# Moving the low part of the FFN's inner rows to another start address in SBUF

## The chip, the cores and the metric

The kernel runs on one core of a Trainium2 chip. The metric is the device time of one execution in microseconds, taken as the median of repeated runs. Before the change it is 2266.62 us (three runs, 2265.76 to 2267.56).

## The reference, cut to what matters

One decoder layer is computed for 256 prompt rows and 32 sample rows, 288 rows together, with a model width of 2048 and an FFN width of 5632:

```python
def ffn_half(h, g, wg, wu, wd):
    hn = rms_norm(h, g)
    return h + 0.5 * ((jax.nn.silu(hn @ wg) * (hn @ wu)) @ wd)

h = ffn_half(h, ...)            # half-step FFN 1
h = mixer_out(h, conv, attn)    # short convolution and forgetting attention, one output projection
h = ffn_half(h, ...)            # half-step FFN 2
h = ple_add(h, p, ...)          # sigmoid gate times a projection of the layer's input embedding
y = rms_norm(h, norm_final)
```

All data is float32. The "inner rows" are `silu(hn @ wg) * (hn @ wu)`, the input of the third FFN product. Only their place in memory is touched here.

## The kernel before, in words

**Three products for one.** The activations lie transposed: 128 features on the partitions, the 288 rows along the free dimension. Each float32 operand of the large products is split into a high part that the matmul's reduced format (float32r) holds exactly and a low part, the rest. A product is then three matmuls that add into one PSUM bank: low activation times high weight, high activation times high weight, high activation times low weight. The first two are line 338 of the profile (`mm<-...,whi`), the third is line 340 (`mm<-...,wlo`). Such a group of three is called a *triplet* below. The activation is the moving operand (128 x 288), the weight the stationary one (128 x 128); every matmul has its own weight load, which runs beside the matmul ahead of it.

**Loops.** `pair` makes two blocks of 128 output features from blocks of 128 input features, four input blocks ("chunk") at a time: for each of the two outputs and each of the four inputs one triplet. Its usual order is low, high, high. The argument `rows_first`, used for the first gate and up pair of FFN 1 while weights still arrive, takes high, low, high, with the same three weights in the order high, high, low.

**The FFN.** The 5632 inner features are 44 blocks. They are made in groups of 6, 6, 8, 8, 8, 8 blocks: for each group the gate and up products with `x` as the moving operand, then the down product over this group's blocks with `hid` as the moving operand, added into `h`. `up` writes a block of `hid`: line 417 (ScalarE) rounds to the high part, line 418 (VectorE) takes the difference. The tile `hid` is made anew for each group, with two buffers.

**Addresses.** A tile's place decides where its parts start. In the built program `hid` begins at byte 129504 of each partition, which is 224 modulo 256, and `x` at byte 38944, which is 32 modulo 256. `both` leaves a gap in front (7 elements for `hid`, 55 for `x`), so that in both the first high part starts at 252 modulo 256. Block k holds the high part, 288 elements or 1152 bytes, and the low part right behind it; a block takes 2304 bytes, nine times 256, so every high part starts at 252 and every low part at 124 modulo 256. The weights' tiles `whi` start at 0 and `wlo` at 224 modulo 256, and a load's columns at multiples of 512 bytes from there. The tiles of the convolution group's output (`zc`) and of the input embedding (`ph`) are made by `both` too, at 252 and 124. The attention group's outputs, `zah` and `zal`, are plain tiles: high parts at 224, low parts at 96.

**The order of work.** The program is recorded by Python loops and placed by a scheduler; TensorE runs its instructions in that order. Weight tiles come in through a queue on SP and are split into `whi` and `wlo` by line 292 (ScalarE and VectorE).

Of the kernel before, what the change touches and what calls it, by code (L numbers as in the profile page):

```python
# [17 lines left out]
F32R = mybir.dt.float32r  # L18
# [7 lines left out]
P = 128  # L26
# [6 lines left out]
NT = SEQ + NS  # L33
# [11 lines left out]
HALVES = 5  # L45
BEFORE_X = 55
BEFORE_W = 7
MANUAL = False
BANKS = dict(mm=3, kt=3, va=2)
KPAIRS = (1, 8, 14, 21, 27, 34, 40, 47)  # L50
# [44 lines left out]
def build(nc, tc, ctx, A, O):  # L95
# [3 lines left out]
    v, s, g, pe, sy = nc.vector, nc.scalar, nc.gpsimd, nc.tensor, nc.sync  # L99
# [99 lines left out]
    def norm_scale(out, squares, width, chunks, load=False):  # L199

        s.activation(sqh, squares, AF.Copy)
        v.tensor_tensor(sql, squares, sqh.bitcast(F32), ALU.subtract)
        defer(lambda: inv_rms(out, [sqh, sql], width, load), chunks)
# [4 lines left out]

    X = {}

    def both(p, name, blocks, before, **k):
        n = blocks * 2 * NT
        whole = 64 if k else 8
        t = p.tile([P, -(-(before + n) // whole) * whole], F32R, name=name, tag=name, **k)
        t = t[:, before:before + n].rearrange("p (k s n) -> p s k n", s=2, n=NT)
        return t[:, 0], t[:, 1]

    def new_x():
        X["hi"], X["lo"] = both(xp, "x", KT, BEFORE_X)

    def make_x(k, gname, work):

        split(X["hi"][:, k, :], X["lo"][:, k, :], h[:, k, :], gain(gname, k))
        squares(k, work)
# [132 lines left out]
    def run_steps():  # L357
        for its, _ in steps:
            items.extend(its)
            for it in its:  # L360
                if it["kind"] == "w":
                    halves.extend((it, j) for j in range(0, it["nk"], 2))
        for i in range(0, 16, 4):
            halves[i + 1], halves[i + 2] = halves[i + 2], halves[i + 1]
        for its, fn in steps:
            load_upto(state["used"] + state["ahead"])
            fn()
            state["used"] += len(its)

    def do(fn):  # L370
        steps.append(([], fn))
# [18 lines left out]
    def ffn(wg, wu, wd, nextgain, work):  # L390
        npairs = DFF // 256
        groups = [range(0, 3), range(3, 6)] + [range(p, p + 4) for p in range(6, npairs, 4)]
        H = {}
        for gi, grp in enumerate(groups):
            firstg = gi == 0 and nextgain == "norm_mix"

            def start():
                H["hi"], H["lo"] = both(work(), "hid", 8, BEFORE_W, bufs=2)
            do(start)
            for pi, pr in enumerate(grp):  # L400
                sg = {}

                def gate(b, o, sg=sg):
                    w = work()
                    t = w.tile([P, NT], F32, name="tg", tag="tg", bufs=2)
                    v.tensor_tensor(t, o, rs, ALU.mult)  # L406
                    u = w.tile([P, NT], F32, name="sg", tag="sg", bufs=2)
                    s.activation(u, t, AF.Silu)  # L408
                    r = w.tile([P, NT], F32, name="sr", tag="sr", bufs=3)
                    g.tensor_tensor(r, u, rs, ALU.mult)  # L410
                    sg[b] = r

                def up(b, o, sg=sg, pi=pi):
                    t = work().tile([P, NT], F32, name="hd", tag="hd", bufs=2)
                    v.tensor_tensor(t, o, sg[b], ALU.mult)  # L415
                    k = 2 * pi + b
                    s.activation(H["hi"][:, k, :], t, AF.Copy)  # L417
                    v.tensor_tensor(H["lo"][:, k, :], t, H["hi"][:, k, :].bitcast(F32), ALU.subtract)  # L418

                lead = firstg and pi == 0  # L420
                gs = pair(wg, pr * 256, list(range(KT)), xact, gate, **(dict(late=4 if lead else 2, tag="va", rows_first=lead) if pr == 0 else {}))
                us = pair(wu, pr * 256, list(range(KT)), xact, up, **(dict(late=4, tag="kt", rows_first=True) if lead else {}))
                steps.extend([x for gu in zip(gs, us) for x in gu] if lead else gs + us)
            k0 = grp[0] * 2
            nb = 2 * len(grp)
            lastg = gi == len(groups) - 1
            for ob in range(KT // 2):
                def down(b, o, ob=ob, lastg=lastg):
                    k = 2 * ob + b
                    v.scalar_tensor_tensor(h[:, k, :], o, 0.5, h[:, k, :], ALU.mult, ALU.add)  # L430
                    if lastg:
                        if k == 0:
                            new_x()
                        make_x(k, nextgain, work())
                steps.extend(pair(wd, ob * 256, list(range(k0, k0 + nb)),
                                  lambda k: (H["hi"][:, k, :], H["lo"][:, k, :]), down, k_of=lambda k, k0=k0: k - k0))
        do(lambda: norm_scale(rs, acc, D, 3, True))
# [484 lines left out]
    def state_in():  # L922
        M["st"] = W["zq"][0].tile([P, CB, DB, 2], F32, name="st")
        M["zc"] = both(W["zq"][0], "zc", CB, BEFORE_W)
        g.dma_start(M["st"].rearrange("p i b t -> p i (b t)"), A["state"])
# [184 lines left out]
    def ple_start():  # L1110
# [4 lines left out]
        g.dma_start(pa, A["p"])  # L1115
        E["hi"], E["lo"] = both(w, "ph", 2, BEFORE_W)
        for k in range(2):
# [61 lines left out]
    do(finish)  # L1179
    with (tc.manual_schedule(engines={mybir.EngineType.PE}) if MANUAL else ExitStack()):  # L1180
        run_steps()
# [67 lines left out]
```

## Time and profile before

| what | us |
|---|---|
| median of three runs | 2266.62 |
| profiled execution, its own time | 2266.11 |
| span of the profiled execution, first to last instruction | 2264.3 |
| TensorE busy in the span | 2250.4 |
| VectorE busy | 1342.5 |
| ScalarE busy | 1047.3 |
| GpSimd busy | 323.0 |

There are 17,387 matmuls in the profile. Of the triplets, 3680 read `x` into the `mm` banks and 1408 read `hid`; `zc` has 128, `zah` and `zal` together 128, `ph` 32, and 160 more read `x` into other banks. A matmul's duration in the profile (290 to 293 ns) is longer than its spacing from the next, because matmuls are pipelined; the time of a stretch is read from starts and counts, not from durations. The timeline prints starts to a hundredth of a microsecond, so a spacing is taken over many matmuls.

### The profile page before, as it was taken

What the parts mean: (1) busy time and instruction counts of PE and PEld (TensorE: products, weight loads), DVE (VectorE), ACT (ScalarE), POOL (GpSimd) and SP (SyncE); (2) the same over time, 40 slices, a digit from 0 to 9 for tenths busy, and PEclk for the clock granted to TensorE, in tenths of its full rate; (3) what the DMA queues carried; (4) which work ended last, traced back from release to release, by engine and by line L of the source; (5) the groups of instructions that cost most, each with busy time, mean ns of one, the idle gap of its engine ahead of it and who ended that gap; (6) DMA issues with size and microseconds to landing.
All of it is one profiled execution on the core that took longest, in us unless ns stands there. A gap on an engine that the chain in (4) does not pass through costs nothing.

```text
span 2264.3 us, 44311 instructions
## 1 busy us (share of the span) xinstructions
PE 2250.4 (99%) x17387; PEld 2194.2 (97%) x17387; DVE 1342.5 (59%) x2413; ACT 1047.3 (46%) x1860; POOL 323.0 (14%) x398
## 2 busy tenths in 40 slices
PE   9999999999999999999999999999999999999997
PEld 9999999999999999888888999999999999999997
DVE  7555555555555586456567875555555555555865
ACT  6444444444444553334344554444444444444654
POOL 1020000000000013345446210000000000000210
PEclk9999999999999999999999999999999999999999
DMA  8575555555555556988988555555555555555552
GB/s 278 169 245 169 170 174 168 168 169 171 172 169 168 168 168 238 332 300 302 331 323 301 167 171 159 179 162 182 168 168 168 174 170 170 168 169 172 169 171 94
DMA packets 342865, 443.37 MB, mean 196 GB/s; under 512 B 17424, under 2 KB 307104, under 8 KB 342656
## 3 DMA queue, kind: packets, MB, share of 16 engines
q1 hardware_dynamic: 320944, 366.25, 50.6%
q0 software_dynamic: 20480, 71.67, 8.9%
q8 instruction: 136, 2.23, 0.4%
q10 hardware_dynamic: 1232, 2.62, 0.3%
q14 instruction: 73, 0.60, 0.1%
HBM read 435.41 MB, written 5.07 MB: 195 GB/s over the span
## 4 chain that ended last, share of the span: by engine, by line
PE 99%; DVE 0%; DMA 0%; issue 0%; ACT 0%; DVEq 0%; ACTq 0%
PE mm L338 61%; PE mm L340 30%; PE va L338 2%; PE va L825 1%; PE va L758 1%; PE va L340 1%; DMA KT<-in_cache_k_dram,idx 0%; PE kt L338 0%; DVE h L1175 0%; PE kt L340 0%; PE kt L879 0%; PE kt L912 0%; PE mm L518 0%; PE kt L903 0%; PE kt L878 0%
## 5 line engine op out<-in xcount | busy, mean ns | idle before, releaser
L338 PE MATMUL mm<-x,whi 128*128 128x288 f32 x7360 | 1438.0, 291 | 0.0
L292 DVE TENSOR_TENSOR wlo<-wraw,whi 128x512 fp32r<-128x512 f32 (+1 forms) x1388 | 974.8, 706 | 748.0 <-ACT whi L292 653.2
L292 ACT ACTIVATE whi<-wraw 128x512 fp32r<-128x512 f32 (+1 forms) x1388 | 862.3, 628 | 881.0 <-PE mm L338 776.9
L338 PEld LDWEIGHTS mm<-x,whi 128*128 128x128 f32 x7360 | 1163.2, 187 | 15.9 <-issue 11.8
L340 PE MATMUL mm<-x,wlo 128*128 128x288 f32 x3680 | 1067.2, 290 | 0.1
L340 PEld LDWEIGHTS mm<-x,wlo 128*128 128x128 f32 x3680 | 689.0, 187 | 0.3 <-DVE wlo L292 0.3
L338 PE MATMUL mm<-hid,whi 128*128 128x288 f32 x2816 | 547.9, 291 | 0.0
L338 PEld LDWEIGHTS mm<-hid,whi 128*128 128x128 f32 x2816 | 445.2, 187 | 0.0
L340 PE MATMUL mm<-hid,wlo 128*128 128x288 f32 x1408 | 408.3, 290 | 0.0
L410 POOL TENSOR_TENSOR sr<-sg,rs 128x288 f32<-128x288 f32 x88 | 71.7, 815 | 1392.8 <-ACT sg L408 1392.6
L340 PEld LDWEIGHTS mm<-hid,wlo 128*128 128x128 f32 x1408 | 263.6, 187 | 0.0
L430 DVE SCALAR_TENSOR_TENSOR h<-mm,h 128x288 f32<-128x288 f32 x192 | 85.8, 454 | 20.0 <-PE mm L340 20.0
L408 ACT ACTIVATE sg<-tg 128x288 f32<-128x288 f32 x88 | 39.0, 444 | 97.7 <-DVE tg L406 97.6
L735 POOL DMA_INDIRECT KT<-in_cache_k_dram,idx x64 | 65.1, 1017 | 129.3 <-DVE idx L166 51.8
L417 ACT ACTIVATE hid<-hd 128x288 fp32r<-128x288 f32 x88 | 39.1, 445 | 92.9 <-DVE hd L415 92.9
L232 POOL TENSOR_TENSOR acc<-acc,sq 128x288 f32<-128x288 f32 x52 | 43.9, 845 | 220.8 <-ACT sq L231 218.3
L259 POOL DMA_INDIRECT page<-in_cache_v_dram,idx x64 | 65.2, 1018 | 63.3 <-PE va L825 42.4
L418 DVE TENSOR_TENSOR hid<-hd,hid 128x288 fp32r<-128x288 f32 x88 | 40.1, 457 | 21.9 <-ACT hid L417 21.9
L338 PE MATMUL mm<-zc,whi 128*128 128x288 f32 x256 | 52.0, 297 | 0.0
L338 PE MATMUL va<-x,whi 128*128 128x288 f32 x256 | 51.2, 293 | 0.0
L415 DVE TENSOR_TENSOR hd<-mm,sr 128x288 f32<-128x288 f32 x86 | 39.0, 454 | 17.1 <-PE mm L340 17.1
L406 DVE TENSOR_TENSOR tg<-mm,rs 128x288 f32<-128x288 f32 x84 | 37.8, 450 | 14.6 <-PE mm L340 13.5
(236 smaller groups left out, 1058.7 us busy)
## 6 DMA issues: line engine op xcount, KB each, us to landing
wraw<-in_w_ffn_gate_dram SPq DMA_DIRECT2D x172, 512.0 KB
wraw<-in_w_ffn_up_dram SPq DMA_DIRECT2D x172, 512.0 KB
wraw<-in_w_ffn_down_dram SPq DMA_DIRECT2D x160, 512.0 KB
wraw<-in_w_in_dram SPq DMA_DIRECT2D x96, 512.0 KB
wraw<-in_w_out_dram SPq DMA_DIRECT2D x32, 512.0 KB
wraw<-in_w_ple_gate_dram SPq DMA_DIRECT2D x32, 512.0 KB
wraw<-in_w_ffn_down_dram SPq DMA_DIRECT2D x32, 256.0 KB
wraw<-in_w_ple_proj_dram SPq DMA_DIRECT2D x8, 256.0 KB
```

The lines of the kernel that those rows point to most:

```text
L232: (v if k >= KT - last_on_v else g).tensor_tensor(acc, acc, sq, ALU.add)
L259: g.indirect_dma_start(out=t, out_offset=None, in_=it["src"], in_offset=bass.IndirectOffsetOnAxis(ap=it["rows"], axis=0))
L292: for i in s.activation(hi, x, AF.Copy), v.tensor_tensor(lo, x, hi.bitcast(F32), ALU.subtract):
L338: pe.matmul(o, hi[:, j % 2, w], x, start=f, stop=False)
L340: state["product"] = pe.matmul(o, lo[:, j % 2, w], xh, start=False, stop=l)
L408: s.activation(u, t, AF.Silu)
L410: g.tensor_tensor(r, u, rs, ALU.mult)
L415: v.tensor_tensor(t, o, sg[b], ALU.mult)
L417: s.activation(H["hi"][:, k, :], t, AF.Copy)
L418: v.tensor_tensor(H["lo"][:, k, :], t, H["hi"][:, k, :].bitcast(F32), ALU.subtract)
L430: v.scalar_tensor_tensor(h[:, k, :], o, 0.5, h[:, k, :], ALU.mult, ALU.add)
L735: d = g.indirect_dma_start(out=t[:, i].rearrange("p h s -> p (h s)"), out_offset=None, in_=A["cache_k"], in_offset=bass.IndirectOffsetOnAx ...
```

## The change

The tile `hid` gets another inner layout. A block takes 640 elements (2560 bytes, ten times 256) and not 576, and the low part starts 337 elements behind the high part and not 288. The high part still starts at 252 modulo 256; the low part starts 1348 bytes behind it, at 64 modulo 256. The gap of 196 bytes between the parts and the rest of the block is not used. A buffer of `hid` grows from 18688 to 20736 bytes, so the second buffer and the FFN's small tiles behind them (`tg`, `sg`, `sr`, `hd`, `sq`) lie 2048 to 4096 bytes further on, at the same residues modulo 256. `x`, `zc` and `ph` go through the same function with its old numbers.

```diff
+FAR = 337
+BLOCK = 640
...
-    def both(p, name, blocks, before, **k):
-        n = blocks * 2 * NT
+    def both(p, name, blocks, before, far=NT, block=2 * NT, **k):
+        n = before + blocks * block
         whole = 64 if k else 8
-        t = p.tile([P, -(-(before + n) // whole) * whole], F32R, name=name, tag=name, **k)
-        t = t[:, before:before + n].rearrange("p (k s n) -> p s k n", s=2, n=NT)
-        return t[:, 0], t[:, 1]
+        t = p.tile([P, -(-n // whole) * whole], F32R, name=name, tag=name, **k)
+        t = t[:, before:n].rearrange("p (k m) -> p k m", m=block)
+        return t[:, :, :NT], t[:, :, far:far + NT]
...
-                H["hi"], H["lo"] = both(work(), "hid", 8, BEFORE_W, bufs=2)
+                H["hi"], H["lo"] = both(work(), "hid", 8, BEFORE_W, FAR, BLOCK, bufs=2)
```

The number of instructions on each engine and their order stay the same. A few waits move, because the scheduler guards memory by where tiles overlap, and some tiles now overlap others. Two of these places follow; line numbers of the changed kernel are higher by two.

On GpSimd, at the end of FFN 1, the forget gate's weights (`wg`) are cleared and the paged log-forget values (`lp`) are fetched. Before:

```order
22 L232 TENSOR_TENSOR acc<-acc,sq 128x288 [waits Activation_49,Pool_49] x12
23 L552 MEMSET wg 128x512 [waits DVE_49,PE_49]
24 L600 DMA lp<-in_cache_logf_dram,pidx 64x1024 [waits DMAHW3_49,DMASW2_49]
25 L941 MEMSET ue 128x2 [waits DVE_49]
26 L941 MEMSET ue 128x2
```

With the change:

```order
22 L234 TENSOR_TENSOR acc<-acc,sq 128x288 [waits Activation_49,Pool_49] x12
23 L554 MEMSET wg 128x512 [waits PE_49]
24 L602 DMA lp<-in_cache_logf_dram,pidx 64x1024 [waits DMASW2_49,DMAHW3_49,DVE_49,PE_49]
25 L943 MEMSET ue 128x2 x2
```

The wait for the last reader of `hid`'s second buffer has gone from the clearing to the fetch behind it.

On VectorE, at the start of FFN 2, the first gate result (`tg`) and the first inner row (`hd`). Before:

```order
1438 L406 TENSOR_TENSOR tg<-va,rs 128x288 [waits DVE_49,PE_49]
1439 L292 TENSOR_TENSOR wlo<-wraw,whi 128x512 [waits PE_49,Activation_49]
1440 L406 TENSOR_TENSOR tg<-va,rs 128x288 [waits PE_49]
...
1448 L415 TENSOR_TENSOR hd<-mm,sr 128x288 [waits DMASW4_49,DMASW3_49,DMASW5_49,PE_49,Pool_49]
1449 L418 TENSOR_TENSOR hid<-hd,hid 128x288 [waits Activation_49]
```

With the change:

```order
1438 L408 TENSOR_TENSOR tg<-va,rs 128x288 [waits DMASW4_49,DMASW3_49,DMASW5_49,DVE_49,PE_49]
1439 L294 TENSOR_TENSOR wlo<-wraw,whi 128x512 [waits PE_49,Activation_49]
1440 L408 TENSOR_TENSOR tg<-va,rs 128x288 [waits PE_49]
...
1448 L417 TENSOR_TENSOR hd<-mm,sr 128x288 [waits PE_49,Pool_49]
1449 L420 TENSOR_TENSOR hid<-hd,hid 128x288 [waits Activation_49]
```

The wait for three of GpSimd's transfer queues has gone from the first `hd` to the first `tg`, ten rows earlier.

## The prediction

> **What bounds the kernel now.** I read the page first: the span, the engines' shares, the chain that ended last.
>
> ```profile
> span 2264.3 us, 44311 instructions
> PE 2250.4 (99%) x17387; PEld 2194.2 (97%) x17387; DVE 1342.5 (59%) x2413; ACT 1047.3 (46%) x1860; POOL 323.0 (14%) x398
> PE 99%; DVE 0%; DMA 0%; issue 0%; ACT 0%; DVEq 0%; ACTq 0%
> ```
>
> TensorE has work in 99% of the span, and the chain runs on it. A busy TensorE is not yet one at its fastest, so the next view is the time by stretch: the two long ones that hold both FFNs, with the granted clock behind the engines.
>
> ```profile
> 30.70:840.00 809.30, 809.30 (x6243) 809.09 (x6242) 470.39 (x789) 377.25 (x650) 57.49 (x69) 1.00 0.56 176
> 1316.70:2150.60 833.90, 833.90 (x6435) 833.90 (x6435) 482.31 (x802) 388.71 (x672) 47.50 (x59) 1.00 0.55 170
> ```
>
> In 809.30 us stand 6243 matmuls without a gap, 129.6 ns each, at full clock. VectorE and ScalarE (third and fourth) are busy for 470 and 377 of 809 us, DMA for 0.56. So here nothing but the spacing of one matmul from the next sets the time. A change can act in two ways only: on that spacing, or by opening a gap.
>
> How many matmuls are concerned, and how long their spacing is, comes from the groups and the timeline.
>
> ```profile
> L338 PE MATMUL mm<-hid,whi 128*128 128x288 f32 x2816 | 547.9, 291 | 0.0
> L340 PE MATMUL mm<-hid,wlo 128*128 128x288 f32 x1408 | 408.3, 290 | 0.0
> ```
>
> 1408 triplets read `hid`, 4224 of 17387 matmuls. One group's down product, first and last rows (start in us, then duration):
>
> ```profile
> 777.92 0.42 PE L338 MATMUL mm<-hid,whi 128*128 128x288 f32 x2
> ...
> 827.69 0.42 PE L338 MATMUL va<-x,whi 128*128 128x288 f32 x2
> ```
>
> Between these starts lie that group's 128 triplets (8 output pairs, two outputs, 8 blocks): 49.77 us / 128 = **388.8 ns a triplet**, which is 129.6 ns a matmul. `hid` now runs at the pace of `x`; all of it is 1408 x 388.8 ns = 547.4 us.
>
> **Does a start address matter at all?** Two stretches of this trace have the same matmul size, the same full queue and other addresses. The attention half of the output projection (low 96, high 224, usual order):
>
> ```profile
> 1266.57 0.29 PE L340 MATMUL mm<-zah,wlo 128*128 128x288 f32 x1
> ...
> 1316.52 0.29 PE L340 MATMUL mm<-zah,wlo 128*128 128x288 f32 x1
> L340 PE MATMUL mm<-zah,wlo x128: 292/292/292, 1266.6 to 1316.5; 128*128 128x288 f32 x128
> ```
>
> 127 triplets in 49.95 us are 393.3 ns each. And the rows-first pair at the kernel's start (the same `x` at 252 and 124, only the three weights in another order):
>
> ```profile
> 20.36 0.29 PE L340 MATMUL va<-x,wlo 128*128 128x288 f32 x1
> ...
> 30.59 0.29 PE L340 MATMUL kt<-x,wlo 128*128 128x288 f32 x1
> L340 PE MATMUL kt<-x,wlo x14: 294/294/294, 20.8 to 30.6; 128*128 128x288 f32 x14
> L340 PE MATMUL va<-x,wlo x13: 294/294/294, 20.4 to 29.8; 128*128 128x288 f32 x13
> ```
>
> 27 third members, so 26 triplets in 10.23 us: 393.5 ns. The pace is therefore not fixed by the 288 columns alone. It takes 388.8 or about 393.4 ns, depending on which starts meet which weights; moving data that is the same (`x`) appears at both paces. What decides between the two can't be read off three cases. The middle figure in such a row (the modelled duration) goes along: 290 in the quicker triplets, 292 and 294 in these.
>
> **The change part by part.**
>
> *The low part's start, 124 to 64.* This touches two of a triplet's three spacings: the one into the low matmul and the one out of it. The third, high to high, keeps its addresses and its weights. What a start at 64 costs, no row shows: all triplets of this program start at 252, 124, 224 or 96. So it is bounded. From above: the slowest triplet seen, 393.5 ns, is 4.7 ns over today's, and 1408 x 4.7 ns = **+6.6 us**. From below: the shortest spacing of full-size weights with more than 128 columns is that of the final row sums.
>
> ```profile
> 2250.52 0.65 PE L1160 MATMUL kt<-acc,meanr 128*128 128x144 f32 x4
> L1160 PE MATMUL kt<-acc,meanr x4: 285/286/286, 2250.5 to 2250.9; 128*128 128x144 f32 x4
> ```
>
> Four take 0.65 us to the last one's end, whose own length is 0.286, so three spacings take 0.36 us, 121 ns each. If both touched spacings fell from 129.6 to 121 ns, that were 1408 x 2 x 8.6 ns = **-24 us**; it is a far bound, since these have half the columns in plain float32. Between the two ends I take **0**: the nearest row is today's `hid` itself, from which the new triplet differs in one start of three, with the same weights in the same order, and the two layouts that do differ in everything are only 1.2% away.
>
> [...]
>
> *The longer block.* Every block is 2560 bytes in place of 2304, both whole multiples of 256, so the residue is the same for all eight blocks, as before. Cost 0.
>
> *The writers.* ScalarE and VectorE write 88 blocks each at the new place:
>
> ```profile
> L417 ACT ACTIVATE hid<-hd x88: 443/445/447, 46.5 to 2089.8; 128x288 fp32r<-128x288 f32 x88
> L418 DVE TENSOR_TENSOR hid<-hd,hid x88: 449/456/461, 47.5 to 2090.3; 128x288 fp32r<-128x288 f32 x88
> ```
>
> Only the low part's writer (L418) has a new address. Were it a tenth slower, 46 ns, it would be hidden: VectorE idles 42% of these stretches, and the block is read only in the group's down product. Only a group's last block could be late, six times in each FFN, for 12 x 0.05 = 0.6 us at most. I take 0.
>
> *The moved waits.* At the end of FFN 1 the fetch of `lp` now waits for the last reader of `hid`, which the clearing ahead of it waited for before.
>
> ```profile
> 827.92 0.53 POOL L552 MEMSET wg<- 128x512 f32 x1 [3.67 <-PE mm L340]
> 828.64 1.41 POOL L600 DMA_INDIRECT lp<-in_cache_logf_dram,pidx  x1 [0.20 <-issue]
> L604 DVE TENSOR_TENSOR_SCAN cum<-consts,lp x8: 386/394/416, 834.9 to 837.8; 64x128 f32<-64x128 f32 x8
> ```
>
> If the clearing goes ahead, the fetch is issued at 827.9 instead of 828.64, and the scans that need it (834.9) come up to 0.7 us sooner, on an engine that isn't the bound; if it doesn't, nothing changes. Behind the fetch on GpSimd's queue stand two small clearings (`ue`), whose tile is next written at 867.9.
>
> ```profile
> L942 POOL COPY ue<-st x8: 192/326/708, 867.9 to 1067.2; 128x16 f32<-128x16 f32 x8
> ```
>
> I take 0, with 0.7 us to either side.
>
> At the start of FFN 2 the first `tg` waits for three of GpSimd's queues in place of the first `hd`.
>
> ```profile
> 1232.02 1.42 POOL L259 DMA_INDIRECT page<-in_cache_v_dram,idx  x1 [0.30 <-issue]
> L406 DVE TENSOR_TENSOR tg<-va,rs x2: 447/448/450, 1328.3 to 1329.9; 128x288 f32<-128x288 f32 x2
> ```
>
> GpSimd issued its last transfer before that point at 1232 us, 96 us earlier. The wait finds its queues done: 0. Had it cost something, the row behind `tg` is a weight split, which TensorE waits for.
>
> *Sum.* 0 on the low part, 0 on the rest: 2266.11 us for the profiled execution's own time (2264.3 us of span and 1.8 us around it). The median of the runs is 0.5 us above it, at 2266.62. I say 2266.4. What a measurement of this kernel can tell from no change is about 0.2%, 4.5 us, which is 3.2 ns a triplet over 1408 triplets.
>
> **The rivals.**
>
> *Slower: the low part falls into the dear pairing.* A triplet then takes the 393.4 ns of the other two layouts, and the time is 2266.4 + 1408 x 4.6 ns = **2272.9 us**. For it: the rows-first pair has exactly today's moving starts and the weights' starts in another order, and that alone costs 4.7 ns. So the pace hangs on how the moving starts stand to the weights' (0 and 224), and 64 is a new distance from both. Against: both high starts and what they meet stay as they are, and the present layout is only one of three, not an exception among many. It decides from 392.1 ns a triplet on.
>
> [...]
>
> *Faster: a start on a multiple of 64 bytes.* 64 is the only start here that is one; 252, 124, 224 and 96 are not. 1152 bytes are 18 pieces of 64: a part that starts at 64 lies in 18, each of the other four in 19. If reading goes by such pieces, the low matmul loses one of 19, 129.6 / 19 = 6.8 ns, and the time is 2266.4 - 1408 x 6.8 ns = **2256.8 us**. For it: all triplets seen have 19 pieces a part, so the gain would be invisible so far, and the row sums' 121 ns show that spacings under 129 exist. Against: no row shows a piece of 64 bytes, and layouts with the same 19 pieces differ by 4.6 ns, so the count isn't what the difference is made of. It decides from 385.6 ns a triplet down.
>
> *The tiles behind `hid` matter.* They move by whole multiples of 256 and are read and written by engines with idle time; it would show as gaps on TensorE, of which these stretches have none. That the parts don't go where the change says is ruled out by the built program's addresses.
>
> **How the numbers follow.** No measurable change 0.55, the faster rival 0.24, the slower one 0.19; the rest, 0.02, is for the tiles behind `hid`, half to each side. That gives faster by over 0.2% 0.25, within 0.2% 0.55, slower 0.20. The likeliest case has a range of its own of 1.6 ns a triplet to either side, 2264.1 to 2268.7 us. The range asked for reaches over both rivals' own times, to 2256 below and 2273.5 above. What it leaves out is a gain on both touched spacings and a loss beyond the slowest layout seen, together about 0.1.
>
> **What would show it.** The same group's down product, from its first low matmul to the next group's first `x`: 49.77 us now; 49.6 to 50.0 if I am right, 50.3 and more for the slower rival, 48.9 and less for the faster. The modelled durations go with it: 290 and 291 on `hid` if nothing changes, 292 to 294 if it is slower, under 290 if it is faster. The triplets of `x` (388.8), of the attention half (393.3) and the gap-free stretches must stay; if the span moves while `hid`'s triplets don't, the cause lies in the moved waits or tiles, and my account of the change is wrong. It is wrong too if the triplets of `hid` move by over 3.2 ns.

## The result and the profile after

| | before | change |
|---|---|---|
| median of the runs, us | 2266.53 (22 runs) | 2263.64 (22 runs) |
| ratio, 95% interval | | 0.9985 (0.9979 to 0.9992) |
| profiled execution, its own time, us | 2266.11 | 2265.26 |
| its span, us | 2264.3 | 2263.5 |
| TensorE busy, us | 2250.4 | 2247.5 |
| a triplet on `hid`, ns | 388.9 | 386.7 |

The kernel is 2.9 us, 0.13%, faster: inside the 0.2% that the forecast called no measurable change. The interval of the ratio leaves out 1, so the gain is clear of the noise. One of the change's runs, 2402.64 us at a granted clock of 0.88 in place of 1.00, stays out of the ratio.

The page of the changed kernel, its span and engines:

```profile
span 2263.5 us, 44314 instructions
PE 2247.5 (99%) x17387; PEld 2191.6 (97%) x17387; DVE 1341.2 (59%) x2413; ACT 1047.2 (46%) x1860; POOL 322.4 (14%) x398
```

TensorE's busy time fell by 2.9 us, the span by 0.8 us only. Where the rest went is seen when the time is cut at the last group of FFN 1 and at the first `hid` matmul of FFN 2. The windows of the changed kernel (stretch and its length, then PE, PEld, DVE, ACT, POOL busy with instruction counts, granted clock, DMA share, GB/s):

```profile
777.59:827.09 49.50, 49.50 (x387) 49.50 (x385) 39.78 (x65) 30.85 (x64) 11.36 (x14) 1.00 0.50 171
827.09:1392.26 565.17, 563.00 (x4408) 509.49 (x4406) 355.81 (x756) 244.50 (x461) 210.48 (x256) 1.00 0.74 261
```

And the same two stretches of the kernel before:

```profile
777.92:827.69 49.77, 49.77 (x386) 49.77 (x385) 39.94 (x65) 30.86 (x64) 10.89 (x13) 1.00 0.52 170
827.69:1391.59 563.90, 563.08 (x4407) 509.54 (x4406) 355.92 (x756) 244.53 (x461) 210.84 (x257) 1.00 0.75 261
```

A down product of 128 triplets takes 49.50 in place of 49.77 us: 386.7 against 388.9 ns a triplet, without a gap in either. The attention stretch has the same busy time (563.0 and 563.1 us) and 1.3 us more idle time in this one execution. The first `hid` matmul also comes 0.9 us later here than before:

```profile
81.97 0.42 PE L340 MATMUL mm<-hid,whi 128*128 128x288 f32 x2
```

It stood at 81.03 us before; in the other kernels' profiles below it stands anywhere from 80.73 to 81.70 us, and at 82.12 us in a second profile of the changed kernel, whose span was 2266.5 us. Experiments 1 and 6, whose programs are the same as the changed one up to this point, have it at 81.54 and 81.16 us, so with one and the same program this start differs by nearly 1 us; the attention stretch, 565.17 us above, took 568.00 us in that second profile. The median over many runs is what counts, and it agrees with the triplets: 1408 x 2.2 ns = 3.1 us.

The groups, the attention half and the two moved waits of the changed kernel:

```profile
L340 PE MATMUL mm<-x,whi 128*128 128x288 f32 x7360 | 1438.0, 291 | 0.0
L340 PE MATMUL mm<-hid,whi 128*128 128x288 f32 x2816 | 544.9, 290 | 0.0
L342 PE MATMUL mm<-hid,wlo 128*128 128x288 f32 x1408 | 408.3, 290 | 0.0
...
L342 PE MATMUL mm<-zah,wlo x128: 292/292/292, 1267.2 to 1317.2; 128*128 128x288 f32 x128
...
827.52 0.97 POOL L602 DMA_INDIRECT lp<-in_cache_logf_dram,pidx  x1 [3.37 <-PE mm L342]
...
L606 DVE TENSOR_TENSOR_SCAN cum<-consts,lp x8: 390/394/414, 833.9 to 836.8; 64x128 f32<-64x128 f32 x8
...
L408 DVE TENSOR_TENSOR tg<-va,rs x2: 450/450/450, 1329.0 to 1330.6; 128x288 f32<-128x288 f32 x2
```

`hid` against `whi` lost 3.0 us; `x` stays at 1438.0, and the duration recorded for the attention half's third members at 292 ns. The fetch of `lp` is issued at 827.52 (828.64 before), its scans start at 833.9 (834.9 before), and neither moves the end. The first `tg` has its two rows 1.6 us apart as before.

From the starts of all 1408 triplets, the mean spacing out of the low matmul fell from 130.0 to 128.3 ns, the one between the two high matmuls from 129.7 to 129.2 ns, and the one into the low matmul stayed at 129.2 ns.

### The profile page after: what moved, and what is told of

Read it like the earlier page. It is cut to its first block, busy times and chain, and to the rows that moved or that the text cites. A ratio compares the mean times of both kernels' runs of the same rounds, so it can differ in the third digit from the quotient of the medians.

```text
span 2263.5 us, 44314 instructions
## 1 busy us (share of the span) xinstructions
PE 2247.5 (99%) x17387; PEld 2191.6 (97%) x17387; DVE 1341.2 (59%) x2413; ACT 1047.2 (46%) x1860; POOL 322.4 (14%) x398
## 4 chain that ended last, share of the span: by engine, by line
PE 98%; DMA 1%; DVE 1%; issue 0%; ACT 0%; SPq 0%; DVEq 0%; POOL 0%; ACTq 0%
PE mm L340 61%; PE mm L342 30%; PE va L340 1%; PE va L827 1%; PE va L760 1%; DMA KT<-in_cache_k_dram,idx 1%; PE va L342 1%; PE kt L340 0%; DVE h L1177 0%; DMA h<-in_x_dram 0%; PE kt L342 0%; PE kt L881 0%; PE kt L914 0%; PE kt L905 0%; PE kt L880 0%
## 5 line engine op out<-in xcount | busy, mean ns | idle before, releaser
L340 PE MATMUL mm<-x,whi 128*128 128x288 f32 x7360 | 1438.0, 291 | 0.0
```

The lines of the kernel that those rows point to most:

```text
L340: pe.matmul(o, hi[:, j % 2, w], x, start=f, stop=False)
```

## The experiments

"(252, 64 | 0, 224)" stands for the starts modulo 256 of high part, low part, `whi` and `wlo`. Each of the scans gives the twelve groups (six in each FFN) twelve different layouts, so that one run tells twelve paces. A group has 96 triplets (the first two of each FFN) or 128. The theories of the expectations, in short: **A**, the pace comes from how the moving starts stand to the weights' starts, so near neighbours behave alike. **B**, reading goes by pieces of 64 bytes. **C**, all starts on multiples of 16 are equally quick. **D**, moving reads and weight loads meet in memory, and four starts that fit together bring a triplet far below 386 ns. **E**, the weight load is a floor, and 386.7 is already on it. **F**, the low start alone decides. **G**, only the starts of the data that moves.

### 1. Twelve low starts

```diff
-FAR = 337
+PLACES = ((7, 337), (7, 336), (7, 338), (7, 341), (7, 345), (7, 349), (7, 289), (7, 305), (7, 321), (7, 329), (7, 288), (7, 297))
...
+                at, far = PLACES[gi if nextgain == "norm_mix" else 6 + gi]
+                H["hi"], H["lo"] = both(work(), "hid", 8, at, far, BLOCK, size=5184, bufs=2)
```

> The twelve groups of the two FFNs get twelve low starts in one kernel, blocks of 2560 bytes and high starts at 252 throughout: 64, 60, 68, 80, 96, 112 in FFN 1 and 128, 192, 0, 32, 124, 160 in FFN 2 (modulo 256). Read: the time of a triplet in each group's down product, against 388.9 ns at 124 and 386.7 ns at 64. Theory A (distance: what counts is how the moving starts stand to the weights' starts, in steps wider than a few elements): 60 and 68 are within 0.5 ns of 64, and the value changes over the circle, with 0 and 32 (next to the weights' 0) among the dear ones, above 388.9. Theory B (multiples of 64 bytes, the prediction's faster rival): 64, 128, 192 and 0 stand at 386.7, all others at 388.9, 60 and 68 among them. Theory C (lines of 16 bytes): all multiples of 16 at 386.7, only 60, 68 and 124 at 388.9.

| low start | 64 | 0 | 124 | 112 | 60 | 80 | 96 | 32 | 192 | 68 | 128 | 160 |
|---|---|---|---|---|---|---|---|---|---|---|---|---|
| ns a triplet | 386.8 | 386.7 | 388.9 | 391.1 | 393.3 | 393.3 | 393.3 | 393.3 | 395.6 | 396.7 | 397.8 | 399.9 |

Windows of this kernel for the starts 60 (96 triplets), 68, 0 and 160 (128 each); the columns are the stretch, its length, PE busy, clock, DMA share, GB/s:

```profile
193.34:231.10 37.76, 37.76 (x290) 1.00 0.63 198
330.66:381.43 50.77, 50.77 (x386) 1.00 0.53 166
1650.11:1699.60 49.49, 49.49 (x386) 1.00 0.54 169
2098.39:2149.58 51.19, 51.19 (x387) 1.00 0.51 164
```

Four bytes to either side of 64 cost 6.6 and 9.9 ns. So A falls in its smooth form. B falls: 128 and 192 lie in 18 pieces of 64 bytes, as 64 and 0 do, and are among the dearest (397.8 and 395.6 ns against 386.8 and 386.7). C falls too: the nine starts on multiples of 16 take 386.7 to 399.9 ns. What is left is a pace that changes sharply with the address, with two good starts among twelve.

### 2. The longer block alone

```diff
-FAR = 337
+FAR = 288
```

> The change with the low part put back: blocks of 2560 bytes, larger buffers, the same moved waits, the low part right behind the high part at 124 modulo 256. If all of the gain is the low start (all theories above): 388.9 ns a triplet and 2266.5 us, ratio to the kernel before 1.000 within 0.0005. If the block, the place of the tiles behind it or the moved waits bring something: below 2265 us at 388.9 ns a triplet, or a triplet under 388 ns.

2266.09 us against 2266.76 us before, ratio 0.9996 (0.9987 to 1.0005), and the old pace. Its last group of FFN 1 and one stage of `x` (256 triplets):

```profile
777.96:827.73 49.77, 49.77 (x386) 49.77 (x385) 39.94 (x65) 30.87 (x64) 11.34 (x14) 1.00 0.52 171
230.40:329.96 99.56, 99.56 (x771) 99.56 (x770) 53.41 (x87) 45.70 (x79) 6.47 (x8) 1.00 0.54 168
```

Block length, the tiles behind `hid` and the moved waits are all in this kernel, and they bring nothing that can be measured. With the changed kernel's 386.7 ns beside this kernel's 388.9, the gain belongs to the low part's start.

### 3. The weights' low part at 0 instead of 224

```diff
-BEFORE_W = 7
+BEFORE_W = 63
...
-    nat = low.tile([P, 40], F32, name="nat")
+    nat = low.tile([P, 48], F32, name="nat")
```

> The change kept, and the low weights' tiles moved from 224 to 0 modulo 256 by 32 unused bytes ahead of them; the moving starts of x (252 and 124), hid (252 and 64) and zc (252 and 124) stay; the attention half's plain tiles go along, from 224 and 96 to 0 and 128. Theory A (distance to the weights' starts): the triplet of x changes although none of its own addresses did, by more than 0.5 ns from 388.9, that is by over 2 us in the span. Theories B and C (only the moving part's own alignment counts): x stays at 388.9 ns and hid at 386.7; by B the attention half, now on multiples of 64, falls from 393.3 ns by 4 ns or more.

The `x` stages between the first and second, and between the second and third group (192 and 256 triplets):

```profile
118.73:193.62 74.89, 74.89 (x579) 74.89 (x578) 40.45 (x66) 34.18 (x59) 13.95 (x14) 1.00 0.63 211
230.74:330.57 99.83, 99.83 (x770) 99.83 (x769) 53.40 (x87) 45.76 (x79) 6.46 (x8) 1.00 0.53 168
```

`x`, whose own place is the old one, went from 388.9 to 390.0 ns; the attention half, now with its high part at 0 and its low part at 128, went from 393.3 to 396.9 ns (B wanted it quicker); `hid` stayed at 386.7. Its one run took 2268.71 us. The weights' start has a say, and not the same one for each layout of the moving data: the time is from one run, the paces are means over a hundred triplets and more.

### 4. Both parts on multiples of 64

```diff
+PLACES = ((56, 288), (8, 288), (24, 288), (40, 288), (8, 320), (8, 336), (24, 320), (24, 304), (56, 336), (40, 304), (40, 320), (56, 320))
```

> Both parts of hid on multiples of 64, weights as they are (high at 0, low at 224). The twelve groups take (high start, low start): (192,64), (0,128), (64,192), (128,0), (0,0), (0,64) in FFN 1 and (64,64), (64,0), (192,0), (128,64), (128,128), (192,192) in FFN 2. Theory D (two terms: a part is read in pieces of 64 bytes, so one that starts on a multiple of 64 takes 18 pieces and not 19, 6.7 ns less; and the moving reads meet the weight load's, which costs a multiple of 3.3 ns by where both start): with two more pieces saved a triplet than at (252,64), some pairs fall to 380 ns or under, down to 373, and others rise, with over 10 ns between the best and the worst; (192,64), whose reads start in the same 64-byte quarter of 256 as today's (252,124), is among the good ones. Theory E (386.7 ns is a floor of the weight load, not of the moving reads): no pair under 386.5 ns. Theory F (only the low start matters): the pairs sort by their low start as in the scan before, 64 and 0 near 386.7, 128 and 192 near 396 to 398, whatever the high start is.

| low \ high | 0 | 64 | 128 | 192 |
|---|---|---|---|---|
| 0 | 396.7 | 399.9 | 393.3 | 400.0 |
| 64 | 393.5 | 397.3 | 393.4 | 393.5 |
| 128 | 400.1 | | 400.0 | |
| 192 | | 400.0 | | 400.0 |

Windows for high 64 with low 192, and high 128 with low 0:

```profile
331.15:382.35 51.20, 51.20 (x387) 1.00 0.51 165
481.90:532.25 50.35, 50.35 (x386) 1.00 0.52 167
```

Every pair on multiples of 64 is dearer than the layout before. The fall that D hoped for does not come, and F is refuted: with low starts 64 and 0, which are the good ones beside a high start of 252, a triplet takes 393.3 to 400.0 ns.

### 5. The same `x`, other weights' starts

`hid` at (0, 128); a tile of weights is 2304 bytes and starts where the group's entry says (four buffers in place of five make room). The first group's `x` stage has gaps here and in experiment 10; its value is from the triplets without one.

```diff
-            hi = wsp.tile([P, 2, 256], F32R, name="whi", tag="whi")
-            lo = wlp.tile([P, 2, 256], F32R, name="wlo", tag="wlo")
+            hi, lo = (p.tile([P, 576], F32R, name=n, tag=n)[:, a:a + 512].rearrange("p (k c) -> p k c", k=2)
+                      for p, n, a in zip((wsp, wlp), ("whi", "wlo"), it["at"]))
```

> hid at (high 0, low 128) in all twelve groups, and the weights' starts changed by group, for that group's gate and up products on x (252,124) too: (high weight, low weight) = (0,224), (0,0), (0,32), (0,64), (32,32), (32,0) in FFN 1 and (32,224), (64,64), (128,128), (128,96), (0,128), (16,16) in FFN 2. Weight tiles are 2304 bytes to make room, with four in place of five of each kind, which may open gaps between matmuls; read are triplets without gaps. Theory D: x, whose own addresses never change, moves by up to 10 ns and more with the weights' starts, and so does hid; two settings that differ by the same shift of both weights differ from each other as a shift of the moving starts would. Theory G (only the moving parts' starts count, the weights' don't): x at 388.9 in all twelve groups; this is already doubtful from the run with the low weights at 0 (390.0).

| `whi`, `wlo` | 0, 224 | 0, 0 | 0, 32 | 0, 64 | 0, 128 | 32, 32 | 32, 0 | 32, 224 | 64, 64 | 128, 128 | 128, 96 | 16, 16 |
|---|---|---|---|---|---|---|---|---|---|---|---|---|
| `x` | 388.9 | 390.0 | 397.8 | 390.0 | 390.0 | 393.4 | 393.3 | 399.9 | 393.3 | 393.3 | 393.4 | 393.3 |
| `hid` | 400.1 | 397.0 | 400.0 | 396.7 | 398.6 | 400.0 | 393.5 | 398.7 | 397.9 | 393.3 | 393.5 | 406.5 |

Two `x` stages of this kernel, 256 triplets each, with weights at (0, 32) and at (0, 64):

```profile
232.87:334.70 101.83, 101.83 (x771) 101.83 (x769) 53.41 (x87) 46.03 (x79) 6.46 (x8) 1.00 0.52 168
385.90:485.74 99.84, 99.84 (x771) 99.84 (x770) 53.30 (x86) 45.48 (x79) 6.46 (x8) 1.00 0.53 170
```

The same `x` at the same address, without a gap, at full clock, and with equal work on the other engines: 397.8 against 390.0 ns. G is refuted, and what D expected of `x` stands: its pace depends on where the weights lie, from 388.9 to 399.9 ns over the twelve groups. The pace goes with the four starts and not with the tile: (0, 128 | 0, 224) takes 400.1 ns here and in experiment 4, and (0, 128 | 0, 0) takes 397.0 ns here and 396.9 in the attention half of experiment 3. What makes the difference between the two rows above, 7.8 ns, is not shown, nor that the reads meet in memory.

### 6. Fewer columns

The interior blocks of each group's down product get 128 to 288 columns, so part of the sum is left out.

```diff
-                        xh, xl = act(k_of(k))
+                        n = NT if k in (kts[0], kts[-1]) else cols
+                        xh, xl = (x[:, :n] for x in act(k_of(k)))
```

> Part of the work is left out: in the down products the first and the last input block run with all 288 columns, the blocks between with fewer, so the sums of the other columns are incomplete. By group, columns 288, 280, 272, 256, 240, 224 in FFN 1 and 192, 160, 128 in FFN 2, all with (high 252, low 64); then 288, 256, 192 with (252, 124). Read: a reduced triplet's time. [...] Theory E (the weight load sets a floor of 128.9 ns a matmul): it stays at 386.7 ns down to 256 columns and lower, and 124 and 64 come together there. [...]

| columns | 288 | 280 | 272 | 256 | 240 | 224 | 192 | 160 | 128 |
|---|---|---|---|---|---|---|---|---|---|
| low at 64, ns a triplet | 386.7 | 381 | 375 | 360 | 336 | 335 | 335 | 335 | 335 |
| low at 124 | 388.9 | | | 351 | | | 336 | | |

Each value is the mean time from the third member of one reduced triplet to that of the next, where two stand side by side without a gap. The timeline of this kernel, third members of successive triplets: two at 256 columns and low 64, then 240, then 256 columns and low 124:

```profile
479.99 0.28 PE L343 MATMUL mm<-hid,wlo 128*128 128x256 f32 x1
...
481.43 0.28 PE L343 MATMUL mm<-hid,wlo 128*128 128x256 f32 x1
...
626.04 0.28 PE L343 MATMUL mm<-hid,wlo 128*128 128x240 f32 x1
...
627.72 0.27 PE L343 MATMUL mm<-hid,wlo 128*128 128x240 f32 x1
...
1949.13 0.28 PE L343 MATMUL mm<-hid,wlo 128*128 128x256 f32 x1
...
1949.83 0.28 PE L343 MATMUL mm<-hid,wlo 128*128 128x256 f32 x1
```

Four triplets in 1.44 us are 360 ns; five in 1.68 us are 336 ns; two in 0.70 us are 350 ns (351 over the whole group). From 240 columns down to 128 a matmul costs about 112 ns with the low part at 64, and so it does at 124 with 192 columns: with the moving data shortened, something that does not depend on the columns is the floor. The weights of 128 columns stay the same in all of them; whether their load or a fixed cost of every matmul is the floor is not shown. At 288 columns a triplet stands 52 ns above this floor, so E's account, that 386.7 is the weight load's own time, is refuted. The paces in question lie above the floor, where the columns still count (386.7 ns at 288, 375 at 272, 360 at 256). At 256 columns the order of the two layouts is turned round (360 against 351 ns), so "64 is better than 124" holds for 288 columns only.

The transposes of 128 columns, 109 ns apart, are no sign of a weight load's own time either. They are plain float32, and in the profile before such matmuls with full weights stand 109 ns apart with 128 columns (line 804), 122 with 144 (line 1160) and 216 to 218 with 256 (lines 912 and 879): 0.84 to 0.85 ns for every column.

### 7. Other high starts, low at 64

```diff
+PLACES = ((6, 338), (5, 339), (4, 340), (23, 321), (55, 289), (39, 305), (9, 335), (0, 344), (15, 329), (31, 313), (16, 328), (47, 297))
```

> The low part of hid at 64 in all groups, the high part at 248, 244, 240, 60, 188, 124 in FFN 1 and 4, 224, 28, 92, 32, 156 in FFN 2. If the good layouts are narrow in the high start as they are in the low one (60 and 68 cost 6.6 and 10 ns more than 64), 248 and 4 are already over 389 ns. If it is a matter of quarters of 64 bytes (252 being the last element of one): 60, 124 and 188 are near 386.7. By the floor theory (E) nothing is under 386.5 ns; a value under it refutes E.

| high start | 156 | 28 | 60 | 188 | 124 | 32 | 92 | 224 | 240 | 248 | 4 | 244 |
|---|---|---|---|---|---|---|---|---|---|---|---|---|
| ns a triplet | 391.1 | 393.3 | 393.3 | 393.3 | 393.4 | 393.4 | 396.7 | 397.7 | 398.3 | 399.9 | 400.1 | 404.8 |

Windows for 248 and 244 (96 triplets each):

```profile
80.84:119.23 38.39, 38.39 (x291) 1.00 0.64 197
193.90:232.76 38.86, 38.86 (x290) 1.00 0.62 193
```

Four bytes below 252 cost 13 ns, eight bytes 18 ns. None of the twelve is as quick as 252, which settles that the high start is as sharp as the low one; starts a quarter or a half of 256 away from 252 (188, 124, 60) are not alike to it.

### 8. and 9. `x` at the same starts as `hid`

`x` in the layout of the change needs room; one buffer fewer for the split weights gives it. Experiment 8 is that buffer alone, experiment 9 both edits.

```diff
-HALVES = 5
+HALVES = 4
...
-        X["hi"], X["lo"] = both(xp, "x", KT, BEFORE_X)
+        X["hi"], X["lo"] = both(xp, "x", KT, BEFORE_X, FAR, BLOCK)
```

> The change with four instead of five tiles of split weights of each kind, so that 4096 bytes come free; nothing else. The weights' and moving starts keep their residues, so triplets stay at 386.7 (hid) and 388.9 ns (x). If the fifth tile is needed anywhere, gaps open before matmuls and it is slower than the change; I expect no gap of weight in the FFNs and within 0.1% of the change, about 2264 us.

> As the run with four tiles of split weights, and x laid out like hid: blocks of 2560 bytes, high part at 252, low part at 64 (the memory comes from the fifth tiles). If the triplet's time goes by the starts alone, x falls from 388.9 to 386.7 ns as hid did: 3680 triplets and 128 more in other banks x 2.2 ns = 8.4 us below the change, about 2255.5 us, ratio to the kernel before 0.995. If x's gain depends on something that hid's stretches do not share (more blocks in a sum, other tiles' traffic), less.

Experiment 8: 2265.68 us against 2267.09 before, ratio 0.9995 (0.9985 to 1.0004), with the change's triplets. The missing buffer costs something, though no gap was expected in the FFNs. Two stretches of experiment 8, ahead of the first down product and around the output projection and the start of FFN 2, then the same two of the change:

```profile
38.60:81.64 43.04, 42.55 (x326) 1.00 0.45 139
1199.07:1325.56 126.49, 126.36 (x970) 1.00 0.64 216
...
39.70:81.97 42.27, 42.27 (x327) 1.00 0.47 148
1199.44:1325.10 125.66, 125.66 (x970) 1.00 0.63 219
```

Each is 0.8 us longer, 1.6 us together, and the first has 0.5 us of idle time where the change has none. Experiment 9: 2258.21 us, ratio 0.9965 (0.9953 to 0.9977), which is above the 2255.5 us and 0.995 that were expected. Its page:

```profile
span 2255.1 us, 44243 instructions
PE 2240.2 (99%) x17387; PEld 2184.3 (97%) x17387; DVE 1343.4 (60%) x2413; ACT 1047.9 (46%) x1860; POOL 322.0 (14%) x398
```

`x` and `hid` now both take 386.7 ns a triplet. The 3840 triplets of `x` at 2.2 ns less are 8.4 us; the medians of experiments 8 and 9, which both lack the buffer, differ by 7.5 us. Data with another content, another tile and another place in memory takes the same pace, 386.7 ns, at the same starts.

### 10. Other weights' starts against (252, 64)

```diff
+PLACES = ((7, 337, 0, 56), (7, 337, 0, 48), (7, 337, 0, 40), (7, 337, 0, 32), (7, 337, 0, 24), (7, 337, 0, 16), (7, 337, 0, 1), (7, 337, 0, 63), (7, 337, 0, 7), (7, 337, 1, 1), (7, 337, 63, 63), (7, 337, 48, 48))
```

> hid as in the change (high 252, low 64) in all groups, the weights' starts changed by group: (high weight, low weight) = (0,192), (0,160), (0,128), (0,96), (0,64), (0,32) in FFN 1 and (0,228), (0,220), (0,252), (4,228), (252,220), (192,160) in FFN 2; x (252,124) sees the same weights in that group's gate and up products. Weight tiles of 2304 bytes, four of each kind. Theory D (how the moving starts stand to the weights' starts): the same moving data runs between 386.7 and about 400 ns as the weights' starts change; low-weight starts on multiples of 64 (192, 128, 64) give 386.7, as 0 did, and 32 to the side (160, 96, 32) do not; (4,228), a shift of 4 bytes, is as dear as the moving starts' shifts by 4 bytes were, 393 ns and more. If one of them is under 386.5 ns, it is the next layout to build. If all stand at 386.7, the weights' starts have nothing to do with it, which the scan before already speaks against.

| `whi`, `wlo` | 0, 220 | 0, 64 | 0, 252 | 0, 192 | 0, 228 | 0, 96 | 0, 160 | 0, 128 | 0, 32 | 4, 228 | 252, 220 | 192, 160 |
|---|---|---|---|---|---|---|---|---|---|---|---|---|
| `hid` (252, 64) | 386.7 | 386.8 | 390.0 | 393.2 | 393.3 | 393.3 | 393.3 | 393.4 | 393.4 | 393.3 | 393.3 | 396.6 |
| `x` (252, 124) | 390.0 | 390.0 | 390.0 | 390.1 | 390.1 | 395.6 | 396.7 | 390.0 | 397.8 | 393.3 | 393.3 | 393.3 |

Windows for (0, 220), 96 triplets, and for both weights 4 bytes further, (4, 228), 128 triplets:

```profile
1516.16:1553.28 37.12, 37.12 (x291) 1.00 0.60 196
1803.72:1854.07 50.35, 50.35 (x386) 1.00 0.52 166
```

Four bytes more for both weights, or for `wlo` alone, cost 6.6 ns, as much as the step from 64 to 60 in the moving data; four bytes less for `wlo` alone cost nothing. Nothing falls below 386.7 ns. That `wlo` be at a multiple of 64 is no rule either: 64 is good (386.8 ns), 128 and 192 are not (393.4 and 393.2).

Nor do the distances between the four starts decide alone. (0, 128 | 0, 224) takes 400.1 ns (experiments 4 and 5), and (252, 124 | 252, 220), the same four starts all 4 bytes lower, takes 393.3 ns here. Common shifts by 32 and by 128 bytes changed little: (224, 96 | 0, 224) and (0, 128 | 32, 0) take 393.3 and 393.5 ns, (128, 0 | 0, 224) and (0, 128 | 128, 96) 393.3 and 393.5 ns.

### 11. and 12. The change, and both tiles, side by side

No new edit: the change, and the kernel of experiment 9, on one chip with the kernel before (2266.60 us).

> The change itself, on the same chip as the next run, so that the two can be compared directly. By its triplets, 1408 x 2.2 ns = 3.1 us below the kernel before: ratio 0.9986.

> x at 252 and 64 too, four tiles of split weights: by the triplets a further 3840 x 2.1 ns = 8.1 us below the change, 11.2 us below the kernel before: ratio 0.9951. If gaps from the smaller number of weight tiles take a part back, about 1 us of it, 0.9955; the first timing gave 0.9965 with an interval of 0.9953 to 0.9977.

The change took 2263.78 us, ratio 0.9989 (0.9980 to 0.9998); with `x` as well 2257.54 us, ratio 0.9959 (0.9945 to 0.9972). Page and an `x` stage (192 triplets) of the latter:

```profile
span 2255.7 us, 44243 instructions
...
118.82:193.06 74.24, 74.24 (x578) 74.24 (x577) 40.80 (x66) 34.17 (x59) 13.35 (x14) 1.00 0.65 216
```

74.24 us / 192 = 386.7 ns. This version is 9.1 us faster than the kernel before and 6.2 us faster than the change. The triplets alone would give 8.4 us over the change; the missing buffer, at 1.6 us in experiment 8, takes most of the difference.

## Why the prediction was right, and where it was not

**The bound.** That only the spacing of the matmuls sets the time of the FFN held: the stretches from which a pace is read are without gaps, and the medians follow the triplets' pace. The other way that it named, opening a gap, was seen where a weight buffer was taken away (experiment 8).

**The low part's start, taken as 0.** The step that was mis-sized: it measured -2.2 ns a triplet, 1408 x 2.2 = -3.1 us (bounds +6.6 and -24 us). The forecast, no measurable change, holds by the 0.2% that it had set, but the time lies 0.5 us below the likeliest case's own range (from 2264.1 us), and the group's 49.50 us just under the 49.6 to 50.0 that were named for it. The reason given for 0, that the new triplet differs from today's in one start of three and so must be near it, was no ground: experiment 1 moved the same one start from 64 by 4 bytes and lost 6.6 and 9.9 ns. With the twelve starts of that experiment, nine would have been slower than before. Zero came near by luck of the start chosen. The upper bound was none: 393.5 ns was the slowest triplet of one program, and four low starts of experiment 1 (68, 128, 160 and 192) take 395.6 to 399.9 ns. The lower bound spoke of something else: the row sums' 121 ns are the price of 144 columns in plain float32 (experiment 6).

**"Two of three spacings."** It failed in its detail. Of the two spacings named only the one out of the low matmul fell (1.7 ns); the one into it stayed, and the untouched one, high to high, fell by 0.5 ns. So, as far as the recorded starts tell, what a matmul costs here is not settled by its own start and its neighbour's alone.

**Block, writers, waits.** All taken as 0. Experiment 2 confirms the block and the waits together: 0.9996 (0.9987 to 1.0005). It has the low part at its old start, so the writer's new place is read from the changed kernel, where a write takes 458 ns in place of 456:

```profile
L420 DVE TENSOR_TENSOR hid<-hd,hid x88: 447/458/462, 48.5 to 2089.7; 128x288 fp32r<-128x288 f32 x88
```

The fetch of `lp` went ahead as its row suggested, and TensorE's next long stage of `x` starts 20.73 us behind the down product in both kernels.

**The slower rival** was right that the weights' starts have a say (experiments 3, 5 and 10). That the pace hangs on how the moving starts stand to the weights' holds only in part: a common shift of all four by 4 bytes changes it by 6.8 ns (experiment 10). Its sign for this layout was wrong: (252, 64 | 0, 224) is among the five quickest found, all at 386.7 or 386.8 ns. And the row that spoke for it was misread. The rows-first pair keeps the weights in their order, high, high, low; what changes places is the high and the low activation ahead of the low weight. So its 4.7 ns stand beside another order of the moving parts, which also puts another weight load beside the low part, and not beside another order of the weights; no run changed that order alone.

**The faster rival** named 64 for a wrong reason. Multiples of 64 as such are not quick: 128 and 192 take 397.8 and 395.6 ns (experiment 1), and high and low starts that are both multiples of 64 take 393.3 to 400.1 ns (experiment 4). With the weights at 0 and 224, 64 and 0 are quick (386.7 or 386.8 ns) beside a high start of 252, and with no other tried (391.1 ns and more, experiments 4 and 7).

**What stays open** is the mechanism. The runs show that four starts together, in steps of 4 bytes, decide the pace at 288 columns (386.7 to 406.5 ns a triplet), which stands above the floor of experiment 6 (335 ns). D's reason, that moving reads and weight loads meet in memory, was not shown: a run of these matmuls without their weight loads was not tried. No rule was found that gives a layout's pace from its starts.

## What to carry to other kernels

Where TensorE runs without gaps, count what a group of matmuls takes from the first start to the next group's first start: a difference of 0.5% in pace shows in one profile, while the kernel's time hides it among gaps that differ by microseconds. If start addresses matter, try a dozen layouts in one run, one for each stage of the same work, and choose moving data and weights together: 4 bytes can cost 13 ns in 387. When a good layout is found, give it to the tile with most of the matmuls first; here that was `x`, worth 6 us beside the 3 us of `hid`, after paying for the buffer that made room.

## What the runs showed of the hardware that was not expected

- The pace of a 128 x 288 matmul stream in float32r varied from 386.7 to 406.5 ns a triplet over 81 combinations of the four starts, at full clock and without gaps. A step of 4 bytes can cost 6.6 to 13 ns, in the high part, the low part or the weights; one such step, `wlo` from 224 to 220, cost nothing.
- Moving data that stays in place changes pace by up to 2.8% (388.9 to 399.9 ns) when only the weights are moved.
- The same four starts all 4 bytes lower changed the pace from 400.1 to 393.3 ns.
- Most of the paces fall on few values, 386.7, 388.9, 390.0, 391.1, 393.3, 395.6, 396.7, 397.8 and 400.0 ns, which are whole multiples of 1.111 ns to about 0.2 ns; six (397.0, 397.3, 398.3, 398.6, 398.7, 404.8) lie between.
- From 240 columns down to 128, the fewest tried, a float32r matmul with its own full weight load costs about 112 ns. Plain float32 costs 0.84 to 0.85 ns a column instead (109 ns at 128, 216 to 218 ns at 256).
- A layout that is better at 288 columns was worse at 256 (360 against 351 ns).
